# Filling products of a routing stage made whole in fp32, and their place in the queues

## The chip, the cores and the metric

The kernel runs on one core of one Trainium2 chip. The metric is the device time of one execution in microseconds; the time of before is the median of three runs.

## The reference

Two model blocks, one after the other, on 512 tokens of 1024 features; all arithmetic is fp32. The change lies in the second half of the first block, a mixture of 16384 single-vector experts (`peer`):

```python
q = einsum('bsd,dq->bsq', h, w_q).reshape(b, s_len, 8, 2, 128)
scores = einsum('bshpc,hpnc->bshpn', q, sub_keys)            # 8 heads x 2 halves x 128 keys
top_s, top_i = top_k(scores, 16)
cand_s = top_s[..., 0, :, None] + top_s[..., 1, None, :]     # 16 x 16 sums a head
cand_i = top_i[..., 0, :, None] * 128 + top_i[..., 1, None, :]
best_s, best_pos = top_k(cand_s, 16)
best_i = take_along_axis(cand_i, best_pos)
gate = softmax(best_s)
...
u = take(expert_u, best_i)                                   # per token: 128 rows of 1024
act = gelu(einsum('td,tkd->tk', h, u))
y = einsum('tk,tkd->td', gate * act, take(expert_v, best_i))
```

## The kernel before

Of the four blocks of 128 tokens, the first gathers its experts' rows by indirect DMA. For the other three the kernel multiplies h with all 16384 expert vectors, as 128 tiles of 128 experts (`u`, 384 tokens wide), and later weighs the results by a dense gate matrix. The first 24 of these `u` tiles need only h, not the routing, so they are laid as filling work into the stages `route` (20 tiles) and `gates` (4 tiles). A generator `ahead` makes them in quarters; `fill.pull(n)` lets n quarters be issued at that place of the program. Each engine works through its own queue in the order in which the program was written there (`manual_schedule`).

fp32 accuracy out of fp32r products: a matrix is cut in a rounded part `hi` (a cast on ScalarE, `whi`, line 151) and the rest `lo` (a subtraction, `wlo`, line 155, on VectorE or GpSimd), and `mm3` (lines 174 to 176) makes the three products lo·hi, hi·lo and hi·hi. `modulated` makes h and its two parts `phh` and `phl`.

`route` has 17 steps. Step i (to 15) makes the query projection of one half head (`mm3`, 24 products of 512 columns into `bank`), copies it (`pqt`), casts and splits the weights of step i + 2, and at its end makes the scores (line 2049) and their copy `sc`. `tail`, run one step later, finds the top 16 of 128 keys for four token blocks on VectorE (`self.top`: maxima, indices, replacement) and casts the indices on ScalarE (`tf`, line 2059). After every second half head `merge` lists the 50 candidate pairs that can be among the best 16 (`cv` the sums of scores, `ci` of indices: seven small additions each, line 2073), finds their top 16, and makes a one-hot `eq`. From it `pick` makes the products with `ci` into the one buffer `pr` (GpSimd, lines 2098 and 2100, for the last head half on VectorE), and `total` sums them on VectorE into the expert numbers `ef` (line 2103). `todo` holds the `pick` and `total` that wait for their place.

A filling tile in `route` is fetched (512 KB), cast by ScalarE and split by GpSimd (the first one cast by VectorE); its result goes through a gelu on ScalarE (`ge`, line 1820). `gates` makes the dense gate matrix from the expert numbers with 384 fp32 products of 128 columns (line 2236).

## Time and profile before

| | |
|---|---|
| median of 3 runs | 3151.77 us (3151.53 to 3152.91) |
| profiled execution, its own time | 3154.18 us |
| its span in the trace | 3152.4 us |
| busy: TensorE, VectorE, ScalarE, GpSimd | 2950.5, 2103.2, 1290.1, 758.4 us |
| `route` (first projection to last sum) | 400.7 to 678.2 us |
| `gates` (start of its first product to start of its last) | 690.6 to 814.2 us |

The span runs from the first to the last instruction of the trace, and all times within it count from its start. An engine's idle time costs something only where the chain that ends last runs through it, so a stage is read by who waits for whom in it, not by shares of busy time.

### The profile page before, as it was taken

The numbers are of one execution on the slowest core, as the hardware profiler recorded it, in microseconds if no ns is written. First come the engines' busy times: TensorE is split into PE (matmuls) and PEld (weight loads), VectorE is DVE, ScalarE is ACT, GpSimd is POOL, SyncE is SP. The second block draws the span as 40 slices with busy tenths as digits, with TensorE's granted clock in tenths as the row PEclk, the third lists the DMA queues.
The fourth block names the chain that finished last, engine by engine and source line by source line (L and its number), as shares of the span: only waits on it lengthen the run. The fifth ranks groups of instructions, "written<-read, shape, count | busy, mean of one in ns | idle before, by whom it ended". The sixth has DMA issues, their size and how long they took to land.

```text
span 3152.4 us, 44761 instructions
## 1 busy us (share of the span) xinstructions
PE 2950.5 (94%) x17073; PEld 2577.2 (82%) x17073; DVE 2103.2 (67%) x4089; ACT 1290.1 (41%) x2356; POOL 758.4 (24%) x805
## 2 busy tenths in 40 slices
PE   8889887758999999999999999999999988999998
PEld 6666576658899999999998777789999966798896
DVE  6775667689777777778776647755445666555454
ACT  3774342237533333333333334433233367433232
POOL 6553244640111211111110145330000332300001
PEclk9999998979999999999999999999999999999999
DMA  6223321215888888888886311022232311122322
GB/s 217 69 81 101 126 77 65 70 51 211 324 316 310 303 313 303 315 309 299 316 308 227 130 64 48 28 74 94 82 100 80 101 33 35 48 95 86 101 89 85
DMA packets 160808, 479.32 MB, mean 152 GB/s; under 512 B 13489, under 2 KB 68657, under 8 KB 142546
## 3 DMA queue, kind: packets, MB, share of 16 engines
q1 hardware_dynamic: 139346, 316.03, 30.1%
q0 software_dynamic: 18432, 134.23, 11.5%
q10 hardware_dynamic: 2816, 26.22, 2.0%
q8 instruction: 134, 2.20, 0.3%
q14 instruction: 80, 0.66, 0.1%
HBM read 449.15 MB, written 27.27 MB: 151 GB/s over the span
## 4 chain that ended last, share of the span: by engine, by line
PE 72%; DVE 12%; issue 6%; POOL 4%; ACT 4%; DMA 1%; SPq 0%; DVEq 0%; POOLq 0%; ACTq 0%
PE big L174 8%; PE big L176 8%; PE big L175 8%; PE y L175 5%; PE y L176 5%; PE y L174 5%; PE u L174 5%; PE u L176 5%; PE u L175 5%; POOL wlo L155 2%; POOL pr L2098 1%; PE bank L2236 1%; PE bank L175 1%; PE bank L176 1%; PE bank L174 1%
## 5 line engine op out<-in xcount | busy, mean ns | idle before, releaser
L155 DVE TENSOR_TENSOR wlo<-wraw,whi 128x1024 fp32r<-128x1024 f32 (+2 forms) x409 | 482.7, 1180 | 532.3 <-ACT whi L151 529.1
L151 ACT CAST whi<-wraw 128x1024 fp32r<-128x1024 f32 (+3 forms) x530 | 524.4, 990 | 702.3 <-PE y L176 267.3
L155 POOL TENSOR_TENSOR wlo<-wraw,whi 128x256 fp32r<-128x256 f32 (+2 forms) x430 | 360.4, 868 | 610.0 <-ACT whi L151 560.4
L174 PE MATMUL big<-xh,wlo 128*128 128x264 f32 (+2 forms) x1408 | 420.7, 299 | 1.3 <-POOL wlo L155 1.3
L174 PE MATMUL u<-phh,wlo 128*128 128x384 f32 x1024 | 353.7, 345 | 70.7 <-ACT sc L2052 31.5
L176 PE MATMUL big<-xh,whi 128*128 128x264 f32 (+2 forms) x1408 | 419.0, 298 | 0.0
L175 PE MATMUL big<-xl,whi 128*128 128x264 f32 (+2 forms) x1408 | 418.1, 297 | 0.0
L1890 POOL DMA_INDIRECT g<-in_uv,idx x128 | 159.8, 1248 | 816.9 <-DVE yg L1904 452.3
L175 PE MATMUL u<-phl,whi 128*128 128x384 f32 x1024 | 349.5, 341 | 0.0
L176 PE MATMUL u<-phh,whi 128*128 128x384 f32 x1024 | 349.2, 341 | 0.0
L176 PE MATMUL y<-whi,ph 128*128 128x512 f32 x768 | 300.8, 392 | 0.0
L175 PE MATMUL y<-wlo,ph 128*128 128x512 f32 x768 | 300.6, 391 | 0.0
L174 PE MATMUL y<-whi,pl 128*128 128x512 f32 x768 | 298.9, 389 | 1.3 <-DVE pl L170 1.3
L174 PEld LDWEIGHTS big<-xh,wlo 128*128 128x128 f32 x1408 | 264.9, 188 | 11.0 <-POOL wlo L155 1.7
L175 PEld LDWEIGHTS big<-xl,whi 128*128 128x128 f32 x1408 | 265.5, 189 | 8.2
L176 PEld LDWEIGHTS big<-xh,whi 128*128 128x128 f32 x1408 | 264.9, 188 | 7.8
L174 PEld LDWEIGHTS u<-phh,wlo 128*128 128x128 f32 x1024 | 197.6, 193 | 81.6 <-POOL wlo L155 46.8
L175 PEld LDWEIGHTS u<-phl,whi 128*128 128x128 f32 x1024 | 197.5, 193 | 4.2
L176 PEld LDWEIGHTS u<-phh,whi 128*128 128x128 f32 x1024 | 197.1, 192 | 0.0
L361 POOL TENSOR_TENSOR acc<-acc,sq 128x528 f32<-128x528 f32 x30 | 47.4, 1580 | 575.5 <-ACT sq L358 575.5
L174 PE MATMUL big<-ah,wlo 128*128 128x264 f32 (+2 forms) x539 | 171.2, 318 | 1.9 <-DVE wlo L155 1.6
L175 PE MATMUL big<-al,whi 128*128 128x264 f32 (+2 forms) x539 | 170.7, 317 | 0.0
(503 smaller groups left out, 6364.3 us busy)
## 6 DMA issues: line engine op xcount, KB each, us to landing
wraw<-in_ut SPq DMA_DIRECT2D x128, 512.0 KB, 5.7
wraw<-in_uv SPq DMA_DIRECT2D x128, 512.0 KB, 5.6
wraw<-in_f_in SPq DMA_DIRECT2D x88, 512.0 KB, 3.4
gscratch<-stage ACTq DMA_DIRECT2D x12, 2048.0 KB, 6.5
gt<-gscratch SPq DMA_DIRECT2D x32, 768.0 KB, 8.2
wada<-in_w_ada SPq DMA_DIRECT2D x40, 512.0 KB, 3.7
wraw<-in_f_out SPq DMA_DIRECT2D x32, 384.0 KB, 3.1
wraw<-in_f_out SPq DMA_DIRECT2D x32, 320.0 KB, 2.9
```

What stands on the lines that cost most here:

```text
L151: self.nc.scalar.copy(hi[:, :n], raw[:, :n])
L155: (engine or self.nc.vector).tensor_tensor(out=lo[:, s], in0=raw[:, s], in1=hi[:, s].bitcast(F32), op=ALU.subtract)
L174: mm(out, lhsT=wl, rhs=xh, start=first, stop=False)
L175: mm(out, lhsT=wh, rhs=xl, start=False, stop=False)
L176: mm(out, lhsT=wh, rhs=xh, start=False, stop=last)
L361: nc.gpsimd.tensor_tensor(out=self.acc, in0=self.acc, in1=sq, op=ALU.add)
L1890: nc.gpsimd.indirect_dma_start(out=g, out_offset=None, in_=t["uv"], in_offset=bass.IndirectOffsetOnAxis(ap=idx[:, k:k + 1], axis=0))
L2098: e.tensor_tensor(out=pr[:, s], in0=eq[:, s], in1=ci[:, s].unsqueeze(3).to_broadcast([P, n, NCAND, PE_K]), op=ALU.mult)
L2236: nc.tensor.matmul(ps[:, e * P:(e + 1) * P], lhsT=b[:, e], rhs=a[:, e], start=e == 0, stop=True, skip_group_check=True)
```

## The change

The 20 filling tiles of `route` are no longer cut in parts. `whole` keeps h in fp32 in the four weight slots (`whi` and `wlo` of the pool `up`) that the parts of the tiles took; a tile is 8 fp32 products of the raw weights with it, instead of 24 fp32r ones. Raw tiles come one ahead, in two slots. The cast and the split of these tiles, and the copies `h2t`, go; from tile 20 on they are cut as before, but the cuts of tiles 21 and 22 come in `gates`, on VectorE, where they were in `route`, on GpSimd. Within a step of `route` the weight split (`lows`) comes behind the top-16 search, the index cast (`casts`) behind the filling quarters; `pick` is issued in the odd step behind the merge and `total` two steps after its `pick`. The last step pulls 11 quarters instead of 3, the end of `route` 4 instead of 12.

```diff
--- before.py
+++ after.py
@@ -141,7 +141,7 @@
         self.nc.sync.dma_start(dst, src)
         return raw
 
-    def cut(self, raw, n, pool=None, engine=None, by_vector=False):
+    def cut(self, raw, n, pool=None, engine=None, by_vector=False, later=None):
         pool = pool or self.wp
         hi = pool.tile([P, 1024], FR, tag="whi", bufs=2, name=self.name("whi"))
         lo = pool.tile([P, 1024], FR, tag="wlo", bufs=2, name=self.name("wlo"))
@@ -150,10 +150,16 @@
         else:
             self.nc.scalar.copy(hi[:, :n], raw[:, :n])
         step = n if engine in (None, self.nc.vector) else 256
-        for a in range(0, n, step):
-            s = slice(a, min(a + step, n))
-            (engine or self.nc.vector).tensor_tensor(out=lo[:, s], in0=raw[:, s], in1=hi[:, s].bitcast(F32),
-                                                     op=ALU.subtract)
+
+        def low():
+            for a in range(0, n, step):
+                s = slice(a, min(a + step, n))
+                (engine or self.nc.vector).tensor_tensor(out=lo[:, s], in0=raw[:, s], in1=hi[:, s].bitcast(F32),
+                                                         op=ALU.subtract)
+        if later is None:
+            low()
+        else:
+            later.append(low)
         return hi, lo
 
     def plan(self, items):
@@ -1148,24 +1154,20 @@
         nc.scalar.activation(sq, self.xT[:, k], AF.Square)
         nc.tensor.matmul(ps, lhsT=c.ones, rhs=sq, start=k == 0, stop=k == KD - 1)
 
-    def modulated(self, rstd, gname, shift, scale, hi, lo, keep=None, bufs=2):
+    def modulated(self, rstd, gname, shift, scale, hi, lo, ts):
         c, nc = self.c, self.c.nc
         a = self.sm.tile([P, KD], F32, tag="ma", name=c.name("ma"))
         nc.vector.scalar_tensor_tensor(out=a, in0=self.mod[:, scale:scale + KD], scalar=1.0, in1=c.col(gname, 0, KD),
                                        op0=ALU.add, op1=ALU.mult)
-        ts = []
 
         def low(k):
             nc.vector.tensor_tensor(out=lo[:, k], in0=ts[k], in1=hi[:, k].bitcast(F32), op=ALU.subtract)
 
         for k in range(KD):
-            t = self.sm.tile([P, S], F32, tag="mt", bufs=bufs, name=c.name("mt"))
-            ts.append(t)
+            t = ts[k]
             nc.vector.tensor_tensor(out=t, in0=self.xT[:, k], in1=rstd, op=ALU.mult)
             nc.scalar.activation(t, t, AF.Identity, scale=a[:, k:k + 1], bias=self.mod[:, shift + k:shift + k + 1])
             nc.scalar.copy(hi[:, k], t)
-            if keep is not None:
-                nc.gpsimd.tensor_copy(keep[:, k], t[:, :P])
             if k > 1:
                 low(k - 2)
         low(KD - 2)
@@ -1787,11 +1789,13 @@
             idx = big.tile([P, NSEL], I32, name="idx")
             ge, uraw, ucut = {}, {}, {}
 
-            EARLY, LATE = 14, STAGES[1] - 1
-            ahead_u = {"fetch": 0, "cut": 0, "by": nc.gpsimd}
+            WHOLE, LATE = 20, STAGES[1] - 1
+            ahead_u = {"fetch": 0, "cut": WHOLE, "by": nc.gpsimd}
+            whole = [up.tile([P, 2, S], F32, tag=tag, bufs=2, name=c.name("h32")) for tag in ("whi", "wlo") for _ in range(2)]
+            whole = [whole[k // 2][:, k % 2] for k in range(KD)]
 
             def spare(u):
-                return c.wp if EARLY + 2 <= u < LATE and u % 2 else up
+                return c.wp if WHOLE <= u < LATE and (u - WHOLE) % 2 == 0 else up
 
             def fetch_u(last):
                 for u in range(ahead_u["fetch"], min(last + 1, P)):
@@ -1801,15 +1805,19 @@
 
             def cut_u(last):
                 for u in range(ahead_u["cut"], min(last + 1, P)):
-                    ucut[u] = c.cut(uraw.pop(u), D, spare(u), ahead_u["by"], u == 0)
+                    ucut[u] = c.cut(uraw.pop(u), D, spare(u), ahead_u["by"])
                     ahead_u["cut"] = u + 1
 
             def u_chunks(u):
-                hi, lo = ucut.pop(u)
+                hi, lo = (uraw.pop(u), None) if u < WHOLE else ucut.pop(u)
                 ps = pu.tile([P, 512], F32, tag="u", name=c.name("u"))
                 for k in range(KD):
-                    c.mm3(ps[:, :TD], hi[:, k * P:(k + 1) * P], lo[:, k * P:(k + 1) * P],
-                          hh[:, k, P:], hl[:, k, P:], k == 0, k == KD - 1)
+                    if lo is None:
+                        nc.tensor.matmul(ps[:, :TD], lhsT=hi[:, k * P:(k + 1) * P], rhs=whole[k][:, P:],
+                                         start=k == 0, stop=k == KD - 1)
+                    else:
+                        c.mm3(ps[:, :TD], hi[:, k * P:(k + 1) * P], lo[:, k * P:(k + 1) * P],
+                              hh[:, k, P:], hl[:, k, P:], k == 0, k == KD - 1)
                     if k % 2 == 1 and k < KD - 1:
                         yield
                 yield lambda: gelu(u, ps)
@@ -1822,10 +1830,13 @@
             def ahead():
                 late = None
                 for u in range(STAGES[1]):
-                    if u < EARLY:
-                        fetch_u(u + 2)
+                    if u < WHOLE - 1:
+                        fetch_u(u + 1)
+                    elif u == WHOLE - 1:
+                        fetch_u(u + 3)
                         cut_u(u + 1)
                     else:
+                        cut_u(u + (u < LATE))
                         fetch_u(min(u + 4, LATE + 1))
                         cut_u(min(u + 3, LATE - (u < LATE - 1)))
                     for x in u_chunks(u):
@@ -1839,8 +1850,7 @@
             fill = Filler(ahead())
             with tc.manual_schedule():
                 fetch_u(1)
-                cut_u(0)
-                self.route(hh, hl, tok, gate, ef, fill)
+                self.route(hh, hl, whole, tok, gate, ef, fill)
                 nc.vector.tensor_copy(idx, ef[:, 0])
                 gep.append(ctx.enter_context(tc.tile_pool(reuse_waits="tile", name="ge2", bufs=STAGES[1] - STAGES[0])))
                 ahead_u["by"] = nc.vector
@@ -2012,7 +2022,7 @@
         for b in range(NB):
             v.max_index(idx[:, b, 8:16], vals[:, b, 8:16], rest[:, b])
 
-    def route(self, hh, hl, tok, gate, ef, fill):
+    def route(self, hh, hl, whole, tok, gate, ef, fill):
         c, nc, t, tc = self.c, self.c.nc, self.c.t, self.c.tc
         with ExitStack() as ctx:
             pre = self.sm = ctx.enter_context(tc.tile_pool(reuse_waits="tile", name="pre", bufs=2))
@@ -2027,8 +2037,7 @@
             sk = pre.tile([P, 16, P], F32, tag="subk", bufs=1, name="subk")
             nc.sync.dma_start(sk, t["sub_keys"])
             wcut = self.wq
-            h2t = pre.tile([P, KD, P], F32, tag="h2t", bufs=1, name="h2t")
-            self.modulated(self.rstd, "g2", 24, 32, hh, hl, h2t, 4)
+            self.modulated(self.rstd, "g2", 24, 32, hh, hl, whole)
             iota = pre.tile([P, NCAND, PE_K], BF, tag="iota", bufs=1, name="iota")
             nc.gpsimd.iota(iota, pattern=[[1, NCAND], [0, PE_K]], base=0, channel_multiplier=0,
                            allow_small_or_imprecise_dtypes=True)
@@ -2056,7 +2065,7 @@
                     ti = pre.tile([P, NB, PE_K], U32, tag="ti", name=c.name("ti"))
                     self.top(pre, ts, ti, sc)
                     tf = pre.tile([P, NB, PE_K], F32, tag="tf", bufs=4, name=c.name("tf"))
-                    nc.scalar.activation(tf, ti, AF.Copy, scale=1.0 if i % 2 else float(PE_N))
+                    casts.append(lambda: nc.scalar.activation(tf, ti, AF.Copy, scale=1.0 if i % 2 else float(PE_N)))
                     tops[i] = (ts, tf)
                 return tail
 
@@ -2104,7 +2113,7 @@
                                             axis=AX.X, op=ALU.add)
                 return pick, total
 
-            tail, todo = None, []
+            tail, todo, lows, casts = None, [], [], []
             for i in range(17):
                 if i < 16:
                     fetch(i + 3)
@@ -2118,21 +2127,25 @@
                     qt = pre.tile([P, S], F32, tag="sq", name=c.name("pqt"))
                     nc.scalar.copy(qt, ps)
                     if i + 2 < 16:
-                        wcut[i + 2] = c.cut(wraw.pop(i + 2), D)
+                        wcut[i + 2] = c.cut(wraw.pop(i + 2), D, later=lows)
                 if tail is not None:
                     tail()
-                if len(todo) == 1 and i < 16:
-                    todo.pop()()
+                while lows:
+                    lows.pop()()
+                if i % 2 and todo:
+                    if len(todo) == 3:
+                        todo.pop(0)()
+                    todo.pop(0)()
                 if i:
-                    fill.pull(4 + (i == 15) - (i == 16))
+                    fill.pull(4 + (i == 15) + 7 * (i == 16))
                 else:
                     for g in range(2):
                         pt = self.bank()
                         for j in range(4):
-                            nc.tensor.transpose(pt[:, j * P:(j + 1) * P], h2t[:, 4 * g + j], c.ident)
+                            nc.tensor.transpose(pt[:, j * P:(j + 1) * P], whole[4 * g + j][:, :P], c.ident)
                         nc.scalar.copy(tok[:, g * 512:(g + 1) * 512], pt)
-                if len(todo) == 2:
-                    todo.pop(0)()
+                while casts:
+                    casts.pop(0)()
                 if i and i % 2 == 0:
                     todo += merge(i // 2 - 1)
                 if i < 16:
@@ -2144,7 +2157,7 @@
             nc.vector.reciprocal(sm, sm)
             nc.vector.tensor_tensor(out=g3, in0=g3, in1=sm.to_broadcast(gsh), op=ALU.mult)
             todo.pop()()
-            fill.pull(12)
+            fill.pull(4)
 
     def gates(self, gate, ef, fill):
         c, nc, tc = self.c, self.c.nc, self.c.tc
```

In the queues this stands as follows. VectorE, steps 6 and 7 of `route` before (an even and an odd one): `wlo` is the weight split, `ts` and `ti` the top-16 search in the scores `sc`, `ef` the sum.

```order
L155 TENSOR_TENSOR wlo_3670<-wraw_3531,whi_3669 128x1024
L2005 MAX ts_3673<-sc_3638 128x8 x4
...
L2013 MAX_INDEX ti_3674<-ts_3673,rest_3675 128x8 x4
L2103 TENSOR_REDUCE ef<-pr_3523 128x4x16
L2073 TENSOR_TENSOR cv_3735<-ts_3564,ts_3673 128x4x16
...
L2073 TENSOR_TENSOR ci_3736<-tf_3587,tf_3696 128x4x16
...
L2088 TENSOR_TENSOR eq_3775<-bf_3773,iota 128x800 x4
L155 TENSOR_TENSOR wlo_3818<-wraw_3640,whi_3817 128x1024
L2005 MAX ts_3821<-sc_3786 128x8 x4
...
L2013 MAX_INDEX ti_3822<-ts_3821,rest_3823 128x8 x4
L155 TENSOR_TENSOR wlo_3927<-wraw_3788,whi_3926 128x1024
```

And in the changed kernel, steps 7 and 8 (an odd and an even one):

```order
L2015 MAX ts_3636<-sc_3602 128x8 x4
...
L2023 MAX_INDEX ti_3637<-ts_3636,rest_3638 128x8 x4
L157 TENSOR_TENSOR wlo_3634<-wraw_3480,whi_3633 128x1024
L2112 TENSOR_REDUCE ef<-pr_3385 128x4x16
L2015 MAX ts_3723<-sc_3689 128x8 x4
...
L2023 MAX_INDEX ti_3724<-ts_3723,rest_3725 128x8 x4
L157 TENSOR_TENSOR wlo_3721<-wraw_3604,whi_3720 128x1024
L2082 TENSOR_TENSOR cv_3762<-ts_3636,ts_3723 128x4x16
...
L2082 TENSOR_TENSOR ci_3763<-tf_3659,tf_3746 128x4x16
...
L2097 TENSOR_TENSOR eq_3802<-bf_3800,iota 128x800 x4
```

The split moved from ahead of the search to behind it, and the sum from the even step, right ahead of the merge, to the end of the odd step.

ScalarE, one step before (the second `whi` is the cast of a filling tile, `ge` a filling tile's gelu) and then after:

```order
L2119 COPY pqt_3815<-bank_3790 128x512
L151 CAST whi_3817<-wraw_3640 128x1024
L2059 ACTIVATE tf_3844<-ti_3822 128x64
L151 CAST whi_3848<-wraw_3699 128x1024
L1820 ACTIVATE ge_3862<-u_3708 128x384
L2052 COPY sc_3895<-bank_3890 128x512
```

```order
L2128 COPY pqt_3718<-bank_3693 128x512
L151 CAST whi_3720<-wraw_3604 128x1024
L1828 ACTIVATE ge_3753<-u_3672 128x384
L2068 ACTIVATE tf_3746<-ti_3724 128x64
L2061 COPY sc_3813<-bank_3808 128x512
```

The filling tile's cast is gone, and the index cast `tf` stands behind the gelu, still ahead of the copy of the scores.

VectorE at the entry of `gates` in the changed kernel, from the route's last sum (`fj` holds the digits of the expert numbers, `hi` and `lo` their one-hots):

```order
L2112 TENSOR_REDUCE ef<-pr_4632 128x4x16
...
L2182 CAST fj<-ij 128x1152
L157 TENSOR_TENSOR wlo_4714<-wraw_4647,whi_4713 128x1024
L157 TENSOR_TENSOR wlo_4722<-wraw_4649,whi_4721 128x1024
L2204 TENSOR_TENSOR hi_4752<-coln,colt 128x256
L2204 TENSOR_TENSOR lo_4753<-coln,colt 128x512
L2230 TENSOR_TENSOR ob_4757<-coln,colt 128x512
```

The two splits `wlo`, of filling tiles 21 and 22, stand between the digits and the one-hots; before, nothing stood there.

## Rows read from the trace of the kernel before

**Rows 1.** Busy time by stretch: two stretches, granted clock behind the engines.
```profile
core 0: us, PE busy (x) PEld busy (x) DVE busy (x) ACT busy (x) POOL busy (x), PEclk, DMA share, GB/s
510.00:540.00 30.00, 23.24 (x110) 21.08 (x111) 20.58 (x112) 7.08 (x12) 16.80 (x16) 0.89 0.19 71
...
690.00:720.00 30.00, 26.19 (x211) 25.16 (x210) 27.84 (x50) 23.36 (x55) 0.00 (x0) 1.00 0.33 141
```

**Rows 2.** Timeline of VectorE, one pair of steps: start, duration, operation.
```profile
485.85 1.62 DVE L155 TENSOR_TENSOR wlo<-wraw,whi 128x1024 fp32r<-128x1024 f32 x1 [3.55 <-ACT whi L151]
...
497.94 2.98 DVE L2103 TENSOR_REDUCE ef<-pr 128x64 f32<-128x1600 f32 x1 [5.78 <-POOL pr L2100]
500.84 0.77 DVE L2073 TENSOR_TENSOR cv<-ts,ts 128x64 f32<-128x64 f32 x7
...
505.63 2.03 DVE L2088 TENSOR_TENSOR eq<-bf,iota 128x800 bf16<-128x800 bf16 x4
507.58 1.22 DVE L155 TENSOR_TENSOR wlo<-wraw,whi 128x1024 fp32r<-128x1024 f32 x1
508.72 0.86 DVE L2005 MAX8 ts<-sc 128x8 f32<-128x128 f32 x4
```

**Rows 3.** Timeline of GpSimd and ScalarE in the same pair.
```profile
486.35 2.54 POOL L2098 TENSOR_TENSOR pr<-eq,ci 128x800 f32<-128x800 bf16 x1
...
496.87 1.04 POOL L2100 TENSOR_TENSOR pr<-pr 128x400 f32<-128x400 f32 x1
...
513.68 1.03 ACT L151 CAST whi<-wraw 128x1024 fp32r<-128x1024 f32 x1
...
514.78 2.79 POOL L155 TENSOR_TENSOR wlo<-wraw,whi 128x256 fp32r<-128x256 f32 x4 [14.09 <-ACT whi L151]
...
515.46 0.60 ACT L2119 COPY pqt<-bank 128x512 f32<-128x512 f32 x1
```

**Rows 4.** Timeline of TensorE: starts of projection, filling tile and scores.
```profile
491.94 0.48 PE L174 MATMUL bank<-phh,wlo 128*128 128x512 f32 x1
...
498.65 0.44 PE L174 MATMUL u<-phh,wlo 128*128 128x384 f32 x1 [0.99 <-POOL wlo L155]
...
502.94 1.05 PE L2049 MATMUL bank<-subk,pqt 128*128 128x128 f32 x8
503.75 0.48 PE L174 MATMUL bank<-phh,wlo 128*128 128x512 f32 x1
```

**Rows 5.** Timeline of TensorE, 372 us: an fp32 product among fp32r ones.
```profile
372.03 1.02 PE L1149 MATMUL norm<-sq,ones 128*128 128x512 f32 x2
372.48 0.79 PE L174 MATMUL bank<-mh,wlo 128*128 128x512 f32 x1
373.12 0.40 PE L175 MATMUL bank<-ml,whi 128*128 128x512 f32 x1
```

**Rows 6.** The page, DMA issues: KB each, median us from issue to landing.
```profile
wraw<-in_ut SPq DMA_DIRECT2D x128, 512.0 KB, 5.7
```

**Rows 7.** Timeline of VectorE and GpSimd: list building while GpSimd multiplies.
```profile
651.68 3.94 DVE L2073 TENSOR_TENSOR cv<-ts,ts 128x64 f32<-128x64 f32 x7
655.55 3.00 DVE L2073 TENSOR_TENSOR ci<-tf,tf 128x64 f32<-128x64 f32 x7
...
657.27 1.05 POOL L2100 TENSOR_TENSOR pr<-pr 128x400 f32<-128x400 f32 x1
```

**Rows 8.** Chain that ended last: scores of steps 0 and 3, then three later pieces.
```profile
413.71 0.89 PE bank L2049 x8
...
445.77 0.89 PE bank L2049 x8
...
621.71 2.95 DVE ef L2103
...
667.31 3.20 POOL pr L2098
...
675.28 2.93 DVE ef L2103
```

## The prediction

> **What bounds the kernel now.** I read the route first as stretches, then engine by engine through one pair of steps, since every second step builds one head's candidate list. In 30 us of the middle of the route no engine is full: TensorE is busy for 23.2 us, VectorE for 20.6, GpSimd for 16.8, ScalarE for 7.1, at a mean granted clock of 0.89 [rows 1]. So the bound is a ring of waits, and VectorE's timeline shows where it waits: 3.55 us ahead of the weight split at 485.85, for ScalarE's cast, and 5.78 us ahead of the sum (`total`) at 497.94, for GpSimd's picks [rows 2]. The ring can be followed once round. The sum runs 497.94 to 500.84 (2.9 us), the list building of `merge` to 507.58 (6.7), the weight split 1.1, the top-16 search from 508.72 until the cast at 513.68 can start (5.0) [rows 2, 3]. ScalarE's in-order queue holds that cast of filling tile u behind the index cast, so it ends near 514.8 (1.1). GpSimd then splits the tile (2.8) and only then makes the pick products, which from 486.35 to 497.91 took 11.6 us [rows 3], and the next sum may start. 2.9 + 6.7 + 1.1 + 5.0 + 1.1 + 2.8 + 11.6 = 31.2 us for a pair; the sums at 497.94 and 621.71 stand four pairs apart, 30.9 us each [rows 2, 8]. The filling tile is thus in the ring, through its cast and split, though nothing in the route needs its result.
>
> **The change, part by part.**
>
> *TensorE.* A filling tile is 24 fp32r products now: 498.65 to 502.94, 4.3 us. The projection of a step is 5.5 us (491.94 to 498.65 less the idle 0.99, less the tail of the last product), the scores 0.8 (502.94 to 503.75) [rows 4]. After, a tile is 8 fp32 products of 384 columns. No row shows one. The nearest is the fp32 product of 512 columns at 372.03, two records long: the fp32r product issued behind it is done with its slot at 373.12, and as that slot is 0.23 us (5.5 / 24), the fp32 product takes 0.86 us [rows 4, 5]. Scaled by columns it is 0.645, the tile 5.2 us. The ends are 4.3 us (no dearer than the three products) and 6.9 (0.86 unscaled); I take 5.2, the row being the same operation. A step is then 5.5 + 5.2 + 0.8 = 11.5 us of TensorE, a pair 23.0, between 21.2 and 26.4 with the ends. So 20 tiles cost some 18 us more TensorE work. It lies beside VectorE's longer pair (26.6 us below); without that cover it would all be seen.
>
> *ScalarE and GpSimd.* Twenty casts of 1.03 us and twenty splits of 2.8 us go, with the eight small copies of h. GpSimd is left with the picks, so they follow the sum that frees their buffer at once. This is what takes 1.1 + 2.8 us out of the ring.
>
> *VectorE's order.* The weight split now stands behind the top-16 search, so its 3.55 us wait falls under that search. The sum stands one odd step later, so that the 5.78 us wait goes: the picks have two steps' work beside them. The index cast (`tf`) stands behind the filling tile's gelu. It still waits for the search, and behind it ScalarE holds the score copy and the next query copy, hence the next scores on TensorE. That wait is cheap while TensorE is a step ahead of VectorE, which its shorter pair lets it be.
>
> *Transfers.* The raw tile u+1 is asked for when tile u starts, a step of over 11 us ahead; landing takes 5.7 us [rows 6], so it is hidden. In step 16, three tiles in a row, the lead is 5.2 us and 0.5 us may show on TensorE, which has time there. On SP's queue only the projection weights, three steps ahead, stand behind it.
>
> *What takes the place of the old waits.* Picks and list building now lie beside each other. Where the trace already has that, the seven additions of `cv` took 3.94 us and those of `ci` 3.00, and `ci` ended as GpSimd's last pick product did, at 658.3 [rows 7]; without GpSimd `cv` takes 0.77 [rows 2]. VectorE's additions and GpSimd's products take turns by whole instructions, so the list is ready only some 0.3 us after the picks end.
>
> The Trainium skill (SBUF — State Buffer, section Who interferes with whom) says this as a rule: a VectorE instruction with two SBUF inputs and a GpSimd instruction that reads SBUF exclude each other for the whole instruction, while `tensor_reduce` never contends. It speaks against this change, whose gain needs the two beside each other. By that rule the pair is the one worked out next; if the two engines only shared bandwidth, the pair would be TensorE's and the time 3095 us. The trace agrees with the rule: 3.94 against 0.77 us.
>
> The new ring is therefore: sum 2.95, picks 11.6 (one weight split cuts in, as at 485.85), `ci` done 0.3 later, rest of the merge 5.4 (6.74 without `cv` and `ci`), search 4.8, split 1.15, and 0.4 for hand-overs: 26.6 us, against 30.9. VectorE has 21.9 us of work in it (31.2 less its two waits of today) and TensorE 23.0. In the pair of steps 13 and 14 no weights are left to split, so 24.4.
>
> **The sum.** *Start.* Steps ran 10.7 us while no picks were there (445.77 less 413.71, over 3 [rows 8]); they become 11.5, and step 0, held by the casts of h, loses about 0.6. Scores of step 3 start at 414.3 + 34.5 = 448.8; scores 0.9, their copy 0.6 and the search 4.8 end at 455.1. The weight split waits for the projection of step 4 (449.6 + 5.5), the query copy 0.6 [rows 3] and the cast 1.0, and ends near 458.2, the merge of head 1 at 464.9, the search of step 4 and its split at 470.9, the sum of head 0 at 473.8. The sum of head 1 ends 26.6 later, at 500.4. Before it ended at 500.9 (497.94 + 2.95). The new order is only level there.
> *Middle.* To the sum of head 5: 3 x 26.6 + 24.4 = 104.2, so 604.6; before 624.7 (621.71 + 2.95). Gain 20.1.
> *End.* Before, the sum of head 7 ends at 678.2 (675.28 + 2.93), 53.5 us after that of head 5 [rows 8], through two more rounds of splits and picks. After: picks of head 6 10.6 (nothing cuts in), `ci` 0.3, small top-16 3.1, exponent 0.7 (an estimate: 512 columns, where 1024 take 1.2 on VectorE), one-hot 2.3, sum 2.95, picks of head 7 8.0 (667.31 to 675.28, both engines at it), sum 2.93, hand-overs 0.3: 31.2. Gain 22.3. The route's last sum ends at 635.8.
> *Gates.* Splits of tiles 21 and 22 move from GpSimd's idle time to VectorE, ahead of the first digits, where VectorE is busy for 27.8 of 30 us [rows 1]: 2 x 1.2 us and one cast to wait for, some 3 us lost, between 1 and 5. Everything behind the gates only starts earlier.
>
> 20.1 + 22.3 - 3 = 39.4 us. The profiled execution took 3154.2 us around its span of 3152.4, so it would take 3114.8. The median is 2.4 lower: **3112**.
>
> **The rivals.**
> *The picks slip in and TensorE becomes the bound.* Steps of 11.5 put the scores of step 15 at 414.3 + 172.5 = 586.8. Its index cast waits behind the gelu of tile 17, 1.75 tiles after those scores, until about 597.6; then 0.7 + 3.1 + 0.7 + 2.3 + 2.95 + 8.0 + 2.93 + 0.3 gives 618.6, a gain of 59.6 - 3 and **3095**. For it: the step's work fits. Against it: rows 7. Chance 0.2.
> *The wait moves into ScalarE's queue.* If TensorE is not far enough ahead, index cast, score copy, query copy, projection cast and weight split make a ring of their own. At 29 us a pair the middle loses 9.6, and **3122**; with 10 us of it in the last steps too, 3132. Chance 0.13. Against it: 3.6 us of slack a pair.
> *Slower: TensorE at its lower clock.* The route already has a granted clock of 0.89. If the fp32 stretches kept TensorE at 1.2 GHz, a step could reach 23 us. Scores of step 15 would have to come near 646 to lose the gain, which is 15.4 us a step, a third of its work at 1.2 GHz; at two thirds (19.2) it is **3208**. Against it: the gates, with fp32 products throughout, have 1.00 [rows 1]. Chance 0.04.
> *No change*, the gain of the middle and end lost again in the gates: chance 0.03; their DMAs and products are not touched.
>
> **How the numbers follow.** The forecast keeps 0.6, with 3104 to 3120 of its own from the gates (1 to 5), the picks (one product more or less a pair) and the start. The range reaches down to TensorE's bound and up into the ScalarE case: 3094 to 3133. 0.2% is 6.3 us, about what a measurement of this kernel can tell from no change. Faster 0.6 + 0.2 + 0.13 = 0.93, same 0.03, slower 0.04.
>
> **What would show it.** Sums 26 to 27 us apart; no GpSimd split and no ScalarE cast of filling tiles until tile 20; `cv` and `ci` stretched to several us in the even steps, ending with the picks; filling tiles of about 5.2 us; the last sum near 636; two splits ahead of the first digits. Sums 23 us apart would show the first rival, a gap ahead of the weight split in the even steps the second, a granted clock of one half in the filling tiles the third.

## The result, and the profile after

The changed kernel takes 3108.36 us (median of 4 runs, 3106.70 to 3109.92) against 3152.32 us (median of 4, 3151.53 to 3152.91). The ratio is 0.9859, with a 95% interval of 0.9848 to 0.9871: 44.0 us faster, where 39.4 had been forecast. Line numbers have moved by 2 to 13: the weight split is L157 now, the filling tile's fp32 product L1816, the scores L2058, the index cast `tf` L2068, the additions of `cv` and `ci` L2082, the one-hot `eq` L2097, the picks L2107 and L2109, the sum L2112.

Busy time by stretch of the kernel after, with the same columns as [rows 1]; the first stretch runs from one sum to the next:

```profile
core 0: us, PE busy (x) PEld busy (x) DVE busy (x) ACT busy (x) POOL busy (x), PEclk, DMA share, GB/s
496.28:522.67 26.39, 26.39 (x113) 19.66 (x112) 26.25 (x119) 5.42 (x10) 11.29 (x8) 1.00 0.25 89
510.00:540.00 30.00, 30.00 (x122) 21.42 (x121) 29.86 (x148) 7.24 (x13) 12.15 (x9) 1.00 0.21 72
```

A pair of steps takes 26.4 us where a pair with weights to split took 31.2 (30.9 on the mean of the four of the prediction). TensorE and VectorE, which stood idle for 7 and 9 of 30 us in [rows 1], seem full, and the granted clock is 1.00 where it was 0.89. The full VectorE needs a second look: its work has not grown by 9 us. Its timeline, start and duration, through the same pair:

```profile
496.28 2.92 DVE L2112 TENSOR_REDUCE ef<-pr 128x64 f32<-128x1600 f32 x1
499.12 0.86 DVE L2015 MAX8 ts<-sc 128x8 f32<-128x128 f32 x4
...
503.80 1.86 DVE L157 TENSOR_TENSOR wlo<-wraw,whi 128x1024 fp32r<-128x1024 f32 x1
505.59 4.38 DVE L2082 TENSOR_TENSOR cv<-ts,ts 128x64 f32<-128x64 f32 x7
509.89 1.63 DVE L2082 TENSOR_TENSOR ci<-tf,tf 128x64 f32<-128x64 f32 x7
...
514.92 2.03 DVE L2097 TENSOR_TENSOR eq<-bf,iota 128x800 bf16<-128x800 bf16 x4
516.86 0.87 DVE L2015 MAX8 ts<-sc 128x8 f32<-128x128 f32 x4
...
521.55 1.22 DVE L157 TENSOR_TENSOR wlo<-wraw,whi 128x1024 fp32r<-128x1024 f32 x1
522.67 2.91 DVE L2112 TENSOR_REDUCE ef<-pr 128x64 f32<-128x1600 f32 x1
```

and GpSimd's timeline beside it:

```profile
499.28 1.56 POOL L2107 TENSOR_TENSOR pr<-eq,ci 128x800 f32<-128x800 bf16 x1 [15.07 <-DVE ef L2112]
...
504.54 2.53 POOL L2107 TENSOR_TENSOR pr<-eq,ci 128x800 f32<-128x800 bf16 x1
...
509.82 1.06 POOL L2109 TENSOR_TENSOR pr<-pr 128x400 f32<-128x400 f32 x1
```

Neither wait of [rows 2] is left: no idle time stands ahead of a split or a sum in these rows. But the seven additions of `cv` take 4.38 us where they took 0.77 alone [rows 2], as in [rows 7], and `ci`, which begins before GpSimd's last product ends at 510.88, ends 0.64 us after it. The wait has become a longer busy time, and a list of waits no longer names it. The ring reads straight from the rows: sum until the picks start 3.0 (496.28 to 499.28), picks 11.6 (to 510.88), `ci` 0.64 later (511.52), the rest of the merge 5.3 (516.86), search 4.7 (521.55), split 1.1 (522.67): 26.4 us.

TensorE's timeline of one step shows the new tile:

```profile
511.77 5.32 PE L1816 MATMUL u<-h,wraw 128*128 128x384 f32 x16
516.93 1.05 PE L2058 MATMUL bank<-subk,pqt 128*128 128x128 f32 x8
517.74 0.48 PE L180 MATMUL bank<-phh,wlo 128*128 128x512 f32 x1
```

Eight products, shown as 16 records, take 5.16 us (511.77 to 516.93); the 24 fp32r products in their place took 4.3 [rows 4]. The step is 11.51 us, so a pair needs 23.0 of TensorE. It is full in this window because it gets ahead of VectorE, by 3.4 us a pair; its first gap comes at 574.6 us. The longest waits between 452 and 600 us, with their sum, count and longest:

```profile
POOL pr L2107 <- DVE ef L2112: 80.1, 5, 20.7
ACT tf L2068 <- DVE ti L2023: 69.5, 10, 14.4
ACT pqt L2128 <- PE bank L182: 34.9, 9, 4.9
...
DVE wlo L157 <- ACT whi L151: 3.3, 2, 1.7
```

VectorE waits 3.3 us in all this time. The two that wait much, GpSimd for the sum and ScalarE for the search, wait for VectorE. The end of the chain that ended last says the same: additions, sums, and only at the very end GpSimd (start, duration):

```profile
505.67 4.30 DVE cv L2082 x7
...
599.55 2.75 DVE ef L2112
...
622.11 3.19 POOL pr L2107
...
630.01 2.86 DVE ef L2112
```

The last sum ends at 632.86 us of the span, 45.3 earlier than in [rows 8]. From there the gain hardly moves: the last product of the expert stage ends 43.4 us earlier (1733.97 against 1777.35), and the span, 3104.9 against 3152.4, is 47.5 shorter.

### The profile page after: what moved, and what is told of

The parts are those of the page before. It is cut to its first block, busy times and chain, and to the rows that moved or that the text cites. A ratio compares the mean times of both kernels' runs of the same rounds, so it can differ in the third digit from the quotient of the medians.

```text
span 3104.9 us, 44278 instructions
## 1 busy us (share of the span) xinstructions
PE 2949.2 (95%) x16913; PEld 2538.5 (82%) x16913; DVE 2118.9 (68%) x4090; ACT 1274.0 (41%) x2337; POOL 690.1 (22%) x709
## 3 DMA queue, kind: packets, MB, share of 16 engines
q1 hardware_dynamic: 139346, 316.03, 30.5%
## 4 chain that ended last, share of the span: by engine, by line
PE 75%; DVE 16%; issue 4%; ACT 3%; POOL 1%; DMA 1%; DVEq 0%; SPq 0%; POOLq 0%; ACTq 0%
PE big L180 9%; PE big L182 8%; PE big L181 8%; PE y L181 6%; PE y L182 6%; PE y L180 5%; PE u L182 5%; PE u L180 5%; PE u L181 5%; PE bank L181 1%; PE bank L182 1%; PE bank L180 1%; PE bank L2249 1%; PE s L545 1%; PE f L180 1%
## 5 line engine op out<-in xcount | busy, mean ns | idle before, releaser
L157 DVE TENSOR_TENSOR wlo<-wraw,whi 128x1024 fp32r<-128x1024 f32 (+2 forms) x411 | 485.4, 1181 | 513.8 <-ACT whi L151 513.4
L151 ACT CAST whi<-wraw 128x1024 fp32r<-128x1024 f32 (+4 forms) x511 | 504.6, 988 | 696.9 <-PE y L182 270.4
L157 POOL TENSOR_TENSOR wlo<-wraw,whi 128x256 fp32r<-128x256 f32 (+1 forms) x342 | 296.1, 895 | 474.9 <-ACT whi L151 454.1
L180 PE MATMUL u<-phh,wlo 128*128 128x384 f32 x864 | 291.7, 338 | 0.6 <-ACT ge L1828 0.6
L182 PE MATMUL u<-phh,whi 128*128 128x384 f32 x864 | 290.4, 336 | 0.0
L181 PE MATMUL u<-phl,whi 128*128 128x384 f32 x864 | 290.0, 336 | 0.0
L182 PE MATMUL big<-ah,whi 128*128 128x264 f32 (+2 forms) x539 | 170.6, 317 | 0.0
L180 PEld LDWEIGHTS y<-whi,pl 128*128 128x128 f32 x768 | 144.6, 188 | 31.8 <-issue 2.9
L182 PEld LDWEIGHTS y<-whi,ph 128*128 128x128 f32 x768 | 144.5, 188 | 30.4
```

The lines of the kernel that those rows point to most:

```text
L151: self.nc.scalar.copy(hi[:, :n], raw[:, :n])
L157: (engine or self.nc.vector).tensor_tensor(out=lo[:, s], in0=raw[:, s], in1=hi[:, s].bitcast(F32), op=ALU.subtract)
L180: mm(out, lhsT=wl, rhs=xh, start=first, stop=False)
L181: mm(out, lhsT=wh, rhs=xl, start=False, stop=False)
L182: mm(out, lhsT=wh, rhs=xh, start=False, stop=last)
```

## The experiments

Nine kernels, each started from the changed kernel unless its diff says otherwise. "Last sum" is when the route's last sum ends in the profiled execution, "experts" when the expert stage's last product ends; for the kernel before these are 678.20 and 1777.35, for the change 632.86 and 1733.97. A pair is the distance of two sums in the middle. Timed beside them, the kernel before had a median between 3152.35 and 3152.43. Ahead of the route the kernels already differ by up to 2 us in code that their edits don't touch (its first projection starts at 399.17 in the change, at 397.26 to 399.21 in the others), so no difference of 2 us or less is given a cause.

| kernel | median us (range) | ratio (95%) | pair | last sum | experts |
|---|---|---|---|---|---|
| e1_sums_back | 3093.14 (3091.43–3095.32) | 0.9810 (0.9796–0.9823) | 23.8 | 618.09 | 1716.56 |
| e2_fp32_only | 3119.90 (3117.34–3122.16) | 0.9896 (0.9880–0.9911) | 27.5 | 645.72 | 1746.88 |
| e3_order_only | 3147.39 (3139.18–3150.29) | 0.9981 (0.9972–0.9990) | 31 | 668.01 | 1767.18 |
| e4_lists_psum | 3095.68 (3090.32–3099.05) | 0.9821 (0.9808–0.9834) | 23.4 | 619.17 | 1720.17 |
| e5_cast_first | 3100.61 (3097.88–3103.03) | 0.9834 (0.9821–0.9848) | 23.8 | 622.44 | 1723.04 |
| e6_split_first | 3116.75 (3111.63–3117.04) | 0.9887 (0.9872–0.9902) | 27.1 | 637.78 | 1736.05 |
| e7_ten_products | 3121.92 (3118.25–3123.07) | 0.9899 (0.9884–0.9914) | 26.6 | 641.56 | 1741.90 |
| e8_gates_pool | 3089.49 (3087.13–3095.39) | 0.9807 (0.9794–0.9820) | 23.8 | 618.04 | 1715.74 |
| e9_eq_whole | 3090.63 (3087.94–3091.96) | 0.9805 (0.9792–0.9819) | 23.0 | 615.25 | 1716.51 |

### Which part of the change bears the gain

**e3_order_only** keeps the split filling tiles of before (cast, GpSimd split, 24 fp32r products) and takes only the new order of split, sum and index cast; **e2_fp32_only** does the opposite (the quarters of the last steps are pulled as in the change).

```diff
 e2: the order of before, round the fp32 tiles
-                    casts.append(lambda: nc.scalar.activation(tf, ti, ...))
+                    nc.scalar.activation(tf, ti, ...)
-                        wcut[i + 2] = c.cut(wraw.pop(i + 2), D, later=lows)
+                        wcut[i + 2] = c.cut(wraw.pop(i + 2), D)
...
-                if i % 2 and todo:
-                    if len(todo) == 3:
-                        todo.pop(0)()
-                    todo.pop(0)()
+                if len(todo) == 1 and i < 16:
+                    todo.pop()()
```

> Only the new order (weight split behind the search, index cast behind the filling quarters, picks first and sums one odd step on); the filling tiles are cut in two parts and split by GpSimd as before. Theory: GpSimd's splits stand behind the picks and take turns with the list building too, so the pair is 26.4 plus 2.8 to 5.6 us, 29 to 32, time 3125 to 3150 us. Rival (the order pays, the fp32 tiles do not): pair near 26.4 us, time 3108 to 3115 us.

> Only the fp32 filling tiles; weight split, index cast, picks and sums in the order of the kernel before (the quarters pulled in the last step as in the changed kernel). Theory: taking cast and split of the filling tile out of the ring is what matters, and the old order keeps picks and list building apart; sum 2.9 + merge 6.7 + picks 12 = 22, below TensorE's 23.0, so pair 23 to 24 us, time 3090 to 3100 us, faster than the whole change. Rival (the new order is what pays): the waits of 3.6 us for ScalarE's cast and of several us for the picks stay, pair 27 to 30 us, time 3115 to 3140 us.

The order alone gains 5 us, the fp32 tiles alone 32.5, and both 44.0. So e2's theory, that the fp32 tiles alone would beat the whole change, missed; its rival's range held. In e3 GpSimd's splits make the tile late and TensorE waits for them. Its waits of that kind between 452 and 600 us, with their sum, count and longest:

```profile
PE u L180 <- POOL wlo L157: 35.1, 5, 10.3
```

In e2 a pair is 27.5 us although no split of a filling tile is left. Here the waits between 452 and 600 us name ScalarE, on both sides:

```profile
PE u L1816 <- ACT ge L1828: 16.6, 6, 4.2
...
DVE wlo L157 <- ACT whi L151: 13.0, 5, 2.6
```

So the old order keeps a ring of its own once the filling tile is out of the first one. Which of its orders does it, e5 and e6 below tell.

### What makes a pair 26.4 us

**e1_sums_back** puts the sum back into the even step, ahead of the merge, so that picks and list building don't stand beside each other. **e4_lists_psum** leaves the order of the change and only puts one operand of every list addition into PSUM.

```diff
 e1
-                if i % 2 and todo:
-                    if len(todo) == 3:
-                        todo.pop(0)()
+                if todo:
                     todo.pop(0)()
...
             todo.pop(0)()
-            todo.pop(0)()
 e4
-            ctx.enter_context(self.psum(bank=6))
+            ctx.enter_context(self.psum(bank=5, lists=1))
...
-                    tops[i] = (ts, tf)
+                    if i % 2:
+                        far = self.ps.tile([P, 2, NB, PE_K], F32, tag="lists", ...)
+                        casts[-1] = lambda: nc.scalar.activation(far[:, 1], ti, AF.Copy)
+                        casts.append(lambda: nc.scalar.copy(far[:, 0], ts))
+                        tops[i] = (far[:, 0], far[:, 1])
+                    else:
+                        tops[i] = (ts, tf)
```

> The changed kernel with one part undone: the sum of a head stands again in the even step, ahead of the merge of the next head, so that the picks lie beside searches and splits and no list building lies beside them. Theory (picks and list building exclude each other by whole instructions, and that alone makes the pair 26.4 us where TensorE needs 23.0): the pair becomes TensorE's 23.0, additions of cv take about 0.8 us again, the last sum near 615 us in the span instead of 633, time about 3091 us. Rival (the pair of 26.4 us is VectorE's and ScalarE's queues, whatever lies beside the picks): the sum waits for the picks again as before the change, pair 26 to 29 us, time 3108 to 3125 us.

> The changed kernel, but the second input of the fourteen list additions (scores and indices of the odd half head) is copied by ScalarE into one PSUM bank, so that they read only one operand from SBUF; order and amount of work on VectorE, GpSimd and TensorE unchanged, one bank fewer for projections and scores. Theory (the additions stand still because GpSimd's products and a VectorE addition with two SBUF operands exclude each other): cv and ci take about 0.8 to 1.2 us each beside the picks instead of 4.4 and 1.6, the pair becomes TensorE's 23.0, time 3093 to 3100 us. Rival (they stand still for another reason: the buffer of the lists, or the picks' own data): cv still 4 us, time within 2 us of the changed kernel, 3108 us.

In e4 the additions stand where they stood in the change, beside the picks; VectorE's timeline, and GpSimd's:

```profile
480.52 0.74 DVE L2088 TENSOR_TENSOR cv<-ts,far 128x64 f32<-128x64 f32 x7
481.18 0.74 DVE L2088 TENSOR_TENSOR ci<-tf,far 128x64 f32<-128x64 f32 x7
```

```profile
479.59 1.89 POOL L2115 TENSOR_TENSOR pr<-pr 128x400 f32<-128x400 f32 x1
481.45 1.54 POOL L2113 TENSOR_TENSOR pr<-eq,ci 128x800 f32<-128x800 bf16 x1
```

0.74 us, against 4.38: with the second operand out of SBUF the two engines don't hold each other, and the pair falls to 23.4. In e1 the additions are fast as well, because nothing runs beside them. But the window of a pair and the timelines of VectorE and GpSimd show what took their place:

```profile
480.20:504.00 23.80, 23.80 (x99) 17.28 (x99) 23.73 (x119) 5.43 (x10) 12.00 (x8) 1.00 0.27 90
```

```profile
482.99 0.79 DVE L2082 TENSOR_TENSOR cv<-ts,ts 128x64 f32<-128x64 f32 x7
...
487.80 4.22 DVE L2097 TENSOR_TENSOR eq<-bf,iota 128x800 bf16<-128x800 bf16 x4
```

```profile
488.52 1.75 POOL L2107 TENSOR_TENSOR pr<-eq,ci 128x800 f32<-128x800 bf16 x1 [11.50 <-DVE eq L2097]
```

The one-hot takes 4.22 us instead of 2.03. It is made block by block, the picks of a block start when its one-hot is done, and the one-hots of the next blocks then take turns with them. Hence VectorE's 23.73 of 23.80 us, and a pair 0.8 above TensorE's 23.0.

**e9_eq_whole** is e1 with the four one-hots in one instruction, which is done before the first pick can start.

```diff
 against e1
-                for b in range(NB):
-                    nc.vector.tensor_tensor(out=eq[:, b], in0=bf[:, b]..., in1=iota, op=ALU.is_equal)
+                nc.vector.tensor_tensor(out=eq, in0=bf.unsqueeze(2).to_broadcast(sh),
+                                        in1=iota.unsqueeze(1).to_broadcast(sh), op=ALU.is_equal)
```

> The kernel of the first experiment with the one-hot of a head made by one VectorE instruction over the four token blocks instead of four, so that GpSimd's first pick can start only when the whole one-hot stands. Theory (in the first experiment GpSimd's picks of the first blocks took turns with the one-hots of the later ones, which took 4.2 us instead of 2.0, and that is why the pair is 23.8 us): the one-hot takes about 2.0 us, VectorE has 21.7 us of work a pair, the pair becomes TensorE's 23.0, the last sum 3 to 4 us earlier than the first experiment's 618 us, time 3088 to 3091 us. Rival (GpSimd starting 1.5 us later costs as much as the turns did): pair 23.8 or more, time 3092 to 3096 us.

The one-hot, GpSimd's first pick behind it, and the window of a pair:

```profile
487.75 1.82 DVE L2096 TENSOR_TENSOR eq<-bf,iota 128x3200 bf16<-128x3200 bf16 x1
```

```profile
489.72 1.55 POOL L2106 TENSOR_TENSOR pr<-eq,ci 128x800 f32<-128x800 bf16 x1 [11.45 <-DVE eq L2096]
```

```profile
480.18:503.20 23.02, 23.02 (x98) 16.88 (x97) 21.67 (x117) 5.42 (x10) 11.24 (x8) 1.00 0.26 93
```

The pair is TensorE's own 23.0 us, and VectorE has 1.35 us to spare in it. The last sum ends 2.8 us earlier than in e1. The expert stage ends level with e1's (1716.51 against 1716.56), so these 2.8 us are not seen at its end: the gates still end 2.9 us earlier, but the first product of VectorE in the expert stage then waits 6.0 us for its gate tile where it waited 4.4 in e1, and where the rest went was not traced. The two medians differ by 2.5 us, with ranges that overlap.

### Which order costs e2 its time

Both take e1 and put one order of before back: **e5_cast_first** the index cast ahead of the gelu, **e6_split_first** the weight split ahead of the search.

```diff
 e5, against e1
-                    casts.append(lambda: nc.scalar.activation(tf, ti, ...))
+                    nc.scalar.activation(tf, ti, ...)
 e6, against e1
-                        wcut[i + 2] = c.cut(wraw.pop(i + 2), D, later=lows)
+                        wcut[i + 2] = c.cut(wraw.pop(i + 2), D)
```

> The kernel of the first experiment (sum back in the even step) with the index cast issued right behind the search again, ahead of the filling tile's gelu on ScalarE. Theory (in the fp32-only kernel the index cast, which waits for VectorE's search, held up the gelu behind it, hence the PSUM bank of the filling tile after next, hence TensorE): waits of TensorE's filling tiles for the gelu come back, TensorE's steps rise from 11.5 to over 12.5 us on the mean, pair 25 to 27.5 us, time 3102 to 3120 us. Rival (the place of the weight split made the fp32-only kernel slow): pair stays near 23.8, time within 3 us of 3093 us.

> The kernel of the first experiment with the weight split ahead of the search again, the index cast left behind the gelu. Theory (the split waits for ScalarE's cast only where TensorE is late, and TensorE is late through the held gelu): TensorE runs ahead at 11.5 us a step, the split finds its cast done in the even steps and waits little in the odd ones, pair 23 to 24.5 us, time 3092 to 3100 us. Rival (the place of the split made the fp32-only kernel slow): VectorE waits some 2.6 us a pair for the cast, pair 26 to 27.5 us, time 3108 to 3120 us.

e5's pairs are the 23.8 us of e1, as its rival has it, and between 455 and 575 us TensorE waits 0.2 us for a gelu. But its time is 7.5 us above e1's, outside the rival's 3: in the last step 27.2 us lie between two sums that stood 22.0 apart. There the theory's mechanism acts after all. The index cast waits 9.5 us for the search, the gelu behind it comes late, and TensorE's filling tile waits for that:

```profile
590.84 2.93 PE L1816 MATMUL u<-h,wraw 128*128 128x384 f32 x4 [5.73 <-ACT ge L1828]
```

The products behind it run at a granted clock of 0.50 (590.5 to 596.5 us), the last scores come late, and VectorE waits 6.0 us for their copy (0.8 in e1). The place of the index cast is therefore worth some 5 us, at the end of the route, and nothing in its pairs. e6 has pairs of 27.1, 3.3 more than e1. VectorE's timeline of e6 at the search, and ScalarE's queue beside it:

```profile
507.12 0.28 DVE L2023 FIND_INDEX8 ti<-ts,rest 128x8 uint32<-128x128 f32 x1
509.63 1.22 DVE L157 TENSOR_TENSOR wlo<-wraw,whi 128x1024 fp32r<-128x1024 f32 x1 [2.23 <-ACT whi L151]
510.77 0.86 DVE L2015 MAX8 ts<-sc 128x8 f32<-128x128 f32 x4
```

```profile
507.44 0.26 ACT L2068 ACTIVATE tf<-ti 128x64 f32<-128x64 uint32 x1 [16.38 <-DVE ti L2023]
507.60 0.57 ACT L2061 COPY sc<-bank 128x512 f32<-128x512 f32 x1
508.07 0.59 ACT L2128 COPY pqt<-bank 128x512 f32<-128x512 f32 x1
508.54 1.06 ACT L151 CAST whi<-wraw 128x1024 fp32r<-128x1024 f32 x1
```

The search ends, then index cast, score copy, query copy and weight cast run one behind the other on ScalarE, 2.2 us, while VectorE stands idle at the split; the next search stands behind the split. That is a ring between the two engines which the place of the split closes and opens, whether the index cast stands ahead of the gelu (e2, 27.5 us) or behind it (e6, 27.1). Of the new order this part earns most: at the end of the expert stage 19.5 us lie between e6 and e1. With the filling tiles still cut and split, the whole new order earned 5.

### How much room TensorE has

**e7_ten_products** issues two of a tile's eight products a second time.

```diff
-                        nc.tensor.matmul(ps[:, :TD], lhsT=hi[...], rhs=whole[k][:, P:], start=k == 0, ...)
+                        for again in range(1 + (k % 4 == 0)):
+                            nc.tensor.matmul(ps[:, :TD], lhsT=hi[...], rhs=whole[k][:, P:],
+                                             start=k == 0 and not again, ...)
```

> The changed kernel with ten fp32 products a filling tile instead of eight (two of them made twice, so the filling tiles' sums are not the reference's): TensorE's step grows from 11.5 to 12.8 us. Theory (VectorE with the picks is the bound at 26.4 us a pair, TensorE has 3.4 us to spare in it): only the first five steps, which TensorE sets, and the last tiles grow, time 4 to 8 us above the changed kernel's, 3112 to 3117 us. Rival (TensorE bounds the route): 20 tiles of 1.3 us more, 3130 to 3136 us.

A step of TensorE becomes 12.8 us, a pair 25.7; the pairs of the route stay at 26.8, 26.7, 26.4 and 26.5. In the middle the 2.6 us a pair are hidden, all but 0.9 us over four pairs. The last sum ends 8.7 us later than in the change: 5.0 up to the first sum, where there are no picks at first and TensorE sets the pace, these 0.9, and 2.8 in the last steps. The experts end 7.9 later, within the theory's 4 to 8, though the median of 3121.92 us lies outside its 3112 to 3117. The two spans lie 16.2 us apart (3121.1 and 3104.9), the medians 13.6; the rest lies behind the expert stage (last section).

### What the gates lost

**e8_gates_pool** is e1 with the splits of tiles 21 to 23 made by GpSimd.

```diff
 against e1
-                ahead_u["by"] = nc.vector
                 scratch = self.gates(gate, ef, fill)
                 fill.drain()
+                ahead_u["by"] = nc.vector
```

> The kernel of the first experiment with the splits of filling tiles 21 to 23 made by GpSimd in the gates stage instead of VectorE. Theory (VectorE's additions with two SBUF operands and GpSimd's take turns by whole instructions): GpSimd's splits, 2.8 us a tile, stop VectorE for about as long as the 1.2 us splits they replace, or longer, time 0 to 5 us above 3093 us. Rival (the gates stage pays only for VectorE's own work): 3 x 1.2 us less, about 3090 us.

The first digits start at 621.94, 4.5 us earlier than in e1, and the last product of the gates ends only 0.7 earlier. GpSimd's splits and a VectorE pass beside them, from the two timelines:

```profile
624.14 9.16 POOL L157 TENSOR_TENSOR wlo<-wraw,whi 128x256 fp32r<-128x256 f32 x8 [7.40 <-ACT whi L151]
```

```profile
626.95 1.23 DVE L2227 TENSOR_TENSOR ob<-coln,colt 128x512 f32<-128x512 f32 x1
```

The one-hot passes of the gates grow from 0.69 to 1.2 us while GpSimd splits beside them, and the 4.5 us are given back within the gates. By the end of the expert stage e8 and e1 are 0.8 us apart, which shows no gain. e8's median of 3089.49 us is where the rival put it, but that is no sign of the rival's reason: three of its five times lie at 3087 to 3089 us and two at 3095, e1's lie between 3091 and 3095, and in the profiled executions the stretch behind the expert stage, which the edit doesn't touch, is 1371.3 us long against e1's 1376.9 (last section).

## Why the prediction was right

**The bound of before.** That the filling tile was in the ring through its cast and split holds: taking them out in e2, with the order left alone, gives 32.5 of the 44.0 us. A pair fell from 31.2 to 27.5 us by it; the two terms of the ring are 1.1 and 2.8. What holds e2's pair at 27.5 is another ring, the one that e6 shows.

**TensorE's price.** The tile measured 5.16 us (5.2 forecast), the step 11.51 (11.5), and it lay beside VectorE's longer pair as said: e7 could add 2.6 us a pair there almost unseen.

**The new ring.** 26.4 us and 24.1 in the pair without a split (26.6 and 24.4). Its working term was the exclusion between list building and picks, and e4 shows the exclusion by removing it: 4.38 us with both operands in SBUF, 0.74 with one in PSUM. This is what the Trainium skill (SBUF — State Buffer, section Who interferes with whom) states for VectorE instructions with two SBUF inputs beside GpSimd instructions that read SBUF. The trace also agrees with what the prediction cites for `tensor_reduce`: the sum `ef<-pr` of the change took 2.85 us with a GpSimd split beside it (630.01 us) and 2.82 with none (619.21).

**Start and end.** The sum of head 1 ended at 499.2 (500.4), that of head 5 at 602.3 (604.6). The end took 30.5 us (31.2), and the last sum ended at 632.9 (635.8). Of these 2.9 us, 1.6 were there ahead of the route's first step, and the first steps gave 0.4 of them back; the rest is 1.1 from the pairs (0.2 to 0.3 each) and 0.7 at the end. Of the 1.6, the change itself accounts for 1.2, which no term of the sum had: the first projection waits 6.50 us for the cast of h where it waited 7.72, and among the experiments only e3, which leaves `modulated` as it was, still waits 7.73.

**The gates, the mis-sized term.** Forecast was a loss of 3, from two splits and one cast. VectorE's timeline after, at the entry to the gates:

```profile
633.04 0.35 DVE L2178 CAST ei<-ef 128x384 int32<-128x384 f32 x1
...
638.91 2.36 DVE L157 TENSOR_TENSOR wlo<-wraw,whi 128x1024 fp32r<-128x1024 f32 x2 [3.79 <-ACT whi L151]
641.19 0.42 DVE L2204 TENSOR_TENSOR hi<-coln,colt 128x256 f32<-128x256 f32 x1
```

and the same two places before:

```profile
678.70 0.89 DVE L2165 CAST ei<-ef 128x384 int32<-128x384 f32 x1
...
684.81 0.42 DVE L2191 TENSOR_TENSOR hi<-coln,colt 128x256 f32<-128x256 f32 x1 [1.64 <-ACT colt L2176]
```

with GpSimd's splits beside it:

```profile
675.21 9.23 POOL L155 TENSOR_TENSOR wlo<-wraw,whi 128x256 fp32r<-128x256 f32 x12
```

The splits cost more than forecast. From the end of the index work (635.12) to the first digits there are 6.1 us, where there were 1.6 before: 4.4 lost, since the splits wait for both casts, which stand behind four copies on ScalarE. But the index work itself takes 2.3 us behind the last sum instead of 5.0, the integer cast 0.35 instead of 0.89: GpSimd no longer splits beside it (its last split there ends at 632.7). Those 2.7 us were in no term of the sum. The two leave 1.7 lost at the first digits, and by the end of the gates 0.2: their last product ends 45.1 us earlier, the last sum 45.3. Where the other 1.5 came back was not traced.

**The rivals.** TensorE as the bound, at 3095, did not come, because the additions did take turns; where e1 and e4 took the turns away, it came at 3093 and 3096. ScalarE's ring, at 3122, did not come either: the new place of the split keeps it open. Its mechanism is real, though: with the split ahead of the search e2 takes 3120 and e6 3117, with pairs of 27.5 and 27.1 us where the rival assumed 29. The lower clock did not come in the stretch that the forecast rests on: 1.00 from 496 to 600 us, where [rows 1] had 0.89 in the middle of the route. At the route's end (612 to 640 us) it is 0.57, while TensorE is busy for 6.7 of 28 us and the chain runs mostly through VectorE and GpSimd. [Rows 1] showed a TensorE that idled 7 of 30 us; the fp32 stretch keeps it at work without a gap, and at the higher level.

The forecast of 3112 came out 3.6 us high. In the profiled executions the gain up to the end of the experts is 43.4 us, 4.0 more than the 39.4 of the sum: 2.9 at the route's end and 2.8 in the gates, less 1.8 at VectorE's first product in the expert stage, which waits 5.9 us for its gate tile where it waited 4.0. Another 4 us that the profiled execution gained behind the expert stage are not shown to be the change's (last section).

## What to carry to other kernels

Work that nobody waits for can still be in the ring of waits, through an in-order queue or a helper engine; making it dearer on an engine with idle time (5.16 against 4.3 us a tile on TensorE) and free everywhere else was worth 32.5 us. When a wait goes, look next at which pairs of operations now stand beside each other: here the wait came back as a longer busy time of VectorE, where no list of waits shows it, and one operand in PSUM (e4), or another order with a one-hot in one piece (e9), gave 13 to 18 us more. The kernel e9, with fp32 tiles, the new place of the split, the sum back ahead of the merge and the whole one-hot, takes 3090.63 us; the times of e1, e4 and e8 overlap with its own, so it is not shown to be the best of these.

## What the hardware showed that was not expected

The stretch behind the expert stage holds the same instructions in every kernel here, yet its length differs by 11 us. The windows from the last expert product to the end, for the change, e4_lists_psum and e7_ten_products:

```profile
1734.00:3104.80 1370.80, 1313.62 (x8955) 1158.75 (x8953) 763.55 (x1493) 529.72 (x1090) 267.09 (x346) 0.98 0.23 74
```

```profile
1720.20:3088.40 1368.20, 1311.70 (x8955) 1156.92 (x8953) 762.97 (x1493) 529.02 (x1090) 267.87 (x346) 0.99 0.24 74
```

```profile
1741.90:3121.00 1379.10, 1322.36 (x8956) 1164.41 (x8953) 763.08 (x1493) 529.27 (x1090) 267.13 (x346) 0.98 0.24 73
```

The busy times of VectorE, ScalarE and GpSimd agree to 0.8 us; TensorE's products differ by 10.7. The granted clock stands at the lower of its two levels (1.2 instead of 2.4 GHz) for 35.7 us of this stretch in e4, 45.3 in the change, 54.8 in the kernel before (1375.1 us long) and 65.4 in e7, and the lengths follow in that order. What sets how long it stands there was not tried. A difference of a few us between two of these kernels is therefore not by itself the price of an edit; the end of the expert stage is the better place to compare them. So 4 us of the change's 47.5 in the two spans, and 8.3 us of the 16.2 by which e7's span is longer than the change's, come from a stretch that no edit touches, and are not shown to be the price of one.
